# Input loads of the attention half of an encoder layer, issued by ScalarE instead of SyncE

## The chip, the cores and the metric

The kernel runs on one core of a Trainium2 chip. A core has a matrix engine (TensorE, PE in the profile, with its weight loads shown apart as PEld), a vector engine (VectorE, DVE), a scalar engine (ScalarE, ACT), a general engine (GpSimd, POOL) and an engine that only issues transfers and waits (SyncE, SP). Each works through its own list of instructions in order; semaphores tie the lists together. Transfers between the core's memory and HBM are run by 16 DMA engines, and an engine's list holds the instruction that issues a transfer, with the waits in front of it.

The metric is device time in microseconds (us) from start to end of one execution; lower is better. Before the change the median of three runs is 1496.47 us (1496.44 to 1498.27).

## The reference, cut to what matters

One layer of a streaming encoder, 1024 positions by 1024 channels, float32. Two kinds of attention run side by side on one normalised input and are joined by one output projection; then a gated MLP follows.

```python
mod = jnp.dot(jax.nn.silu(c), w_ada[l]) + b_ada[l]
sh_a, sc_a, g_a, sh_m, sc_m, g_m = jnp.split(mod, N_MOD, axis=-1)
h = modulate(rmsnorm(x, g_attn_norm[l]), sh_a, sc_a)
proj = jnp.dot(h, w_in[l])
q_lat, kv_lat, k_rope, ca_qkv = jnp.split(proj, split_pts, axis=-1)
q = jnp.dot(rmsnorm(q_lat, g_q_latent[l]), w_q_up[l]).reshape(B, S, MLA_HEADS, MLA_QK)
kv = jnp.dot(rmsnorm(kv_lat, g_kv_latent[l]), w_kv_up[l]).reshape(B, S, MLA_HEADS, MLA_NOPE + MLA_V)
...
o_mla = mla_attention(q, k, v)                       # 8 heads, chunk-causal, all earlier keys
...
o_ca = chunk_attention(cq, ck, cv, rel_bias[l])      # 8 heads, band of 9 chunks of 64 keys, bias
mixed = jnp.dot(jnp.concatenate([o_mla, o_ca], axis=-1), w_out[l])
x = x + g_a[:, None, :] * mixed
h = modulate(rmsnorm(x, g_mlp_norm[l]), sh_m, sc_m)
u = causal_dwconv(jnp.dot(h, w_up[l]), conv_w[l], conv_b[l])
gate, val = jnp.split(u, 2, axis=-1)
x = x + g_m[:, None, :] * jnp.dot(jax.nn.silu(gate) * val, w_down[l])
```

Inputs x and c, the positions and all weights come from HBM; the result goes back to HBM.

## The kernel before, in words

**Arithmetic.** Every large product keeps float32 accuracy by splitting both operands into a rounded high part and a low remainder and adding three matmuls (`gemm3`, lines 146 to 152; its lines 150, 151 and 152 are the matmuls of most rows of the profile). So each weight that is loaded raw is then split: ACT writes the high part (`hi_of`, line 75), POOL or DVE subtracts it for the low part (`lo_of`, line 82). The raw buffer is free again when that subtraction is done.

**Stages.** (1) 0 to about 65 us: x is loaded and normalised, the first modulation rows are computed, and the query/key projection of the first pair of heads runs. (2) To about 105 us: the rotary tables (`rope_tables`), on DVE. (3) About 105 to 435 us: the banded attention, four pairs of heads. (4) About 435 to 690 us: the latent attention (`mla`), eight heads. (5) To about 790 us: output projection, residual, second normalisation. (6) The MLP, to the end, with its own loads at lines 978, 1023 and 1027.

**The attention loop.** `Unit.scores` (line 636) does 128 queries of one head: score matmuls (line 658), a minimum over the row on DVE (673 or 677), the exponential on ACT (683), the reciprocal and scale on DVE (685, 686), the probabilities as a float16 high part on POOL (helper line 71) and a low part on DVE (703), and then a transposing transfer issued by SP (705). `Unit.values` (709) multiplies the transposed tile with the values (716); it comes `DEPTH` = 3 tiles later. At the end of a group of four tiles the head's output goes to HBM (line 725, SP). There are three transpose buffers (`PT_BUFS` = 3).

**Work put between the tiles.** `pace` (line 805) takes steps from a list of fillers, which give PE work while a tile waits for the other engines: value and query/key projections (`f_v`, `f_qk`, by `load_w`), the latent projections (`f_m`, also by `load_w`), their up-projections (`f_up`), and the output projection of the four finished banded head pairs (`f_oca`). A side list, `f_ada` (419), computes three more modulation rows: 96 loads of 128 KB (line 426), each followed by one multiply-add of DVE (lines 428 and 430).

**The loads that the change touches** (all on SP before), with the buffer that each waits for:

- line 184 in `load_w`: 64 loads of projection weights into a ring `wr` of three buffers;
- line 263: the positions, once;
- line 426 in `f_ada`: 96 loads, in a ring `A` of three buffers that also holds the running sum;
- line 454 in `gate_bcast`: 6 short bias rows (4 from `f_ada`, 2 from the MLP's `gate_row`);
- lines 526 and 532 in `f_up`: 6 loads of up-projection weights, and line 591 in `load_wo`: 16 loads of output weights of 256 KB, all in a ring `sq` of two buffers that the squares of the normalisation use as well;
- line 604 in `f_oca`: 16 loads of 256 KB, the banded heads' outputs, written to HBM earlier at line 725, in a ring `R` of four;
- line 733 in `load_bias`: 8 bias tables, a ring of two.

**What sets the order.** The program text gives the dependencies and priorities; the order of each engine's list is then made by a planner that plays the program through with modelled durations before it is built:

```python
with tile.TileContext(nc, schedule_with_timeline_sim=True) as tc, ExitStack() as ctx:
...
            with tc.high_priority(offset=OFF_S):
```

`high_priority` lifts the score, probability and value steps ahead of the fillers (lines 645, 684, 714). A load's place in its engine's list is thus where the planner expects its buffer to come free, and the list is then fixed.

Of the kernel before, what the change touches and what calls it, by code (L numbers as in the profile page):

```python
# [23 lines left out]
P = 128  # L24
# [38 lines left out]
def layer_kernel(ctx, tc, I, out):  # L63
# [3 lines left out]
    def f32(ap):  # L67
        return ap.bitcast(F32)
# [101 lines left out]
    def load_w(name, src, ncol, he="a", ssw=None):  # L170
        tiles = []
        for k in range(ND):
            if ncol <= 256:
                w = hw.tile([P, 2, 256], F32R, name=f"{name}s{k}", tag="ws", bufs=16)
                hi, lo = w[:, 0, :ncol], w[:, 1, :ncol]
            else:
                wh = hw.tile([P, 512], F32R, name=f"{name}h{k}", tag="ws", bufs=16)
                wl = hw.tile([P, 512], F32R, name=f"{name}l{k}", tag="ws", bufs=16)
                hi, lo = wh[:, :ncol], wl[:, :ncol]
            for c0 in range(0, ncol, 256):  # L180
                c = slice(c0, min(c0 + 256, ncol))
                raw = hw.tile([P, 256], F32, name=f"{name}r{k}_{c0}", tag="wr", bufs=3)
                rw = raw[:, :c.stop - c0]
                sp.dma_start(rw, src[:, k, c])
                if ssw is not None:
                    junk = qtile(f"{name}j{k}")
                    act.activation(junk[:, :c.stop - c0], rw, AF.Square, accum_out=ssw[:, k:k + 1])
                hi_of(he, hi[:, c], rw)
                lo_of("p", lo[:, c], rw, hi[:, c])
            tiles.append((hi, lo))  # L190
        return tiles
# [44 lines left out]
    for d in range(ND):  # L236
        if d + 1 < ND:
            load_ada(d + 1)
        w = wada[d]
# [20 lines left out]


    def rope_tables():
        sp.dma_start(pos_i[:], I["pos"])
        buf = [st.tile([P, 8, NT, 16], F32, name=f"rt{i}", tag="x", bufs=4) for i in range(8)]
        cnt = [0]

        def T():
            cnt[0] += 1
            return buf[(cnt[0] - 1) // 8][:, (cnt[0] - 1) % 8]

        def rnd(src, q):
            o = T()
            dve.tensor_scalar(o, src, q, MAGIC, op0=MUL, op1=ADD)
            dve.tensor_scalar(o, o, MAGIC, None, op0=SUB)
            return o

        def fma(n, c, b):
            o = T()
            dve.scalar_tensor_tensor(o, n, c, b, op0=MUL, op1=ADD)
            return o  # L280

        p1 = _grid(TWO_PI, 2.0 ** -9)
        p2 = _grid(TWO_PI - p1, 2.0 ** -21)
        p3 = TWO_PI - p1 - p2

        def reduce(src):
            n = rnd(src, 1.0 / TWO_PI)
            r = fma(n, -p1, src)
            r = fma(n, -p2, r)
            return fma(n, -p3, r)  # L290

        pf = cst.tile([P, NT], F32, name="pf")
        dve.tensor_copy(pf[:], pos_i[:])
        ang = T()
        dve.tensor_tensor(ang, pf[:].unsqueeze(2).to_broadcast([P, NT, 16]),
                          pk[:, C_INV:C_INV + 16].unsqueeze(1).to_broadcast([P, NT, 16]), op=MUL)
        nh = rnd(ang, 2.0 ** -20)
        rem = fma(nh, -(2.0 ** 20), ang)
        nm = rnd(rem, 2.0 ** -8)
        lo = fma(nm, -(2.0 ** 8), rem)  # L300
        tot = reduce(lo)
        for n, w in ((nh, 2.0 ** 20), (nm, 2.0 ** 8)):
            c = w - round(w / TWO_PI) * TWO_PI
            c1 = _grid(c, 2.0 ** -9)
            x = T()
            dve.tensor_scalar(x, n, c1, None, op0=MUL)
            x = fma(n, c - c1, reduce(x))
            y = T()
            dve.tensor_tensor(y, tot, x, op=ADD)
            tot = y  # L310
        tot = reduce(tot)
        pi_s = 3.1415925
        sn, cn, cl, c2, cl2 = T(), T(), T(), T(), T()
        dve.tensor_scalar(cl, tot, pi_s, -pi_s, op0=MIN, op1=MAX)
        act.activation(sn, cl, AF.Sin)
        dve.tensor_scalar(c2, tot, math.pi / 2, None, op0=ADD)
        dve.tensor_scalar(cl2, reduce(c2), pi_s, -pi_s, op0=MIN, op1=MAX)
        act.activation(cn, cl2, AF.Sin)

        for tab, c0 in ((tabq, C_RQ), (tabk, C_RK)):  # L320
            for half, trig in ((0, cn), (1, sn)):
                for j in range(2):
                    o = half * 32 + j * 16
                    dve.tensor_tensor(tab[:, :, o:o + 16], trig,
                                      pk[:, c0 + j * 16:c0 + j * 16 + 16].unsqueeze(1)
                                      .to_broadcast([P, NT, 16]), op=MUL)
# [92 lines left out]
    def f_ada():  # L419
        for m in (2, 3, 4):  # L420
            for n in range(4):
                acc = atile(f"aacc{m}_{n}")
                c0 = m * D + n * 256
                for k in range(ND):
                    w = atile(f"aw{m}_{n}_{k}")
                    sp.dma_start(w[:], I["w_ada"][k * P:(k + 1) * P, c0:c0 + 256])
                    if k == 0:
                        dve.tensor_scalar(acc[:], w[:], cs[:, 0:1], None, op0=MUL)
                    else:
                        dve.scalar_tensor_tensor(acc[:], w[:], cs[:, k:k + 1], acc[:], op0=MUL, op1=ADD)  # L430
                    if k % 2 and k < ND - 1:
                        yield 0
                yield 0
                yield 0
                pt = ps.tile([P, 512], F32, name=f"p_ada{m}_{n}", tag="mm", bufs=2)
                if m == 2:
                    gate_bcast(pt[:, :256], acc, c0, 256, atile)
                    g = atile(f"gab{n}")
                    act.activation(g[:], pt[:, :256], AF.Copy)
                    sp.dma_start(ga_d[:, n * 256:(n + 1) * 256], g[:])  # L440
                else:
                    for i in range(2):
                        pe.matmul(pt[:, i:i + 1], acc[:, i * P:(i + 1) * P], ones[:, 0:1], start=True, stop=True)
                    act.activation(modT[:, 3 if m == 3 else 2, 2 * n:2 * n + 2], pt[:, 0:2], AF.Copy)
                yield 0
        b = pk[:, C_B + 24:C_B + 40].rearrange("p (a b) -> p a b", a=2)
        dve.tensor_tensor(modT[:, 3, :], modT[:, 3, :], b[:, 0], op=ADD)
        dve.tensor_tensor(modT[:, 2, :], modT[:, 2, :], b[:, 1], op=ADD)
        dve.scalar_tensor_tensor(modT[:, 2, :], modT[:, 2, :], 1.0, pk[:, C_GM:C_GM + ND], op0=ADD, op1=MUL)

    def gate_bcast(pt, acc, c0, w, alloc):

        br = alloc(f"brow{c0}")
        sp.dma_start(br[0:1, :w], I["b_ada"][:, c0:c0 + w])
        dve.tensor_tensor(acc[0:1, :w], acc[0:1, :w], br[0:1, :w], op=ADD)
        pe.matmul(pt, ones[:], acc[:, :w], start=True, stop=True)

# [59 lines left out]
    def f_up(gr):  # L517
# [5 lines left out]
        wq = []  # L523
        for k in range(2):
            raw = qtile(f"wqr{gr}_{k}")
            sp.dma_start(raw[:, :384], I["w_qu"][gr][:, k, :])
            w = g4([P, 2, 512], F32R, f"wq{gr}_{k}")
            hi_of("a", w[:, 0, :384], raw[:, :384])
            lo_of("p", w[:, 1, :384], raw[:, :384], w[:, 0, :384])
            wq.append(w)  # L530
        raw = qtile(f"wkr{gr}")
        sp.dma_start(raw[:], I["w_kvu"][gr])
        ssw = cst.tile([P, 1], F32, name=f"sswm{gr}")
        junk = qtile(f"wkj{gr}")
        act.activation(junk[:, 0:256].rearrange("p (a b) -> p a b", a=4),
# [50 lines left out]
    def load_wo(k0, n, he, le):  # L586
        ws = []
        for k in range(k0, k0 + 4):
            raw = qtile(f"wor{k}_{n}")
            sl = slice(n * 512, (n + 1) * 512)  # L590
            sp.dma_start(raw[:], I["w_out"][k * P:(k + 1) * P, sl])
            w = g4([P, 2, 512], F32R, f"wo{k}_{n}")
            hi_of(he, w[:, 0], raw[:])
            lo_of(le, w[:, 1], raw[:], w[:, 0])
            ws.append(w)
        return ws

    def f_oca():
        for n in range(2):
            ws = load_wo(4, n, "a", "p")  # L600
            for t in range(NT):
                lo = rtile(f"cl{t}_{n}", (P, 4, P), F32R)
                hi = rtile(f"ch{t}_{n}", (P, 4, P), F32R)
                sp.dma_start(f32(lo[:]), oT_d[4:8, :, t * P:(t + 1) * P].rearrange("k p t -> p k t"))
                hi_of("a", hi[:], f32(lo[:]))
                lo_of("p", lo[:], f32(lo[:]), hi[:])
                pt = ps.tile([P, 512], F32, name=f"oc{t}_{n}", tag="mm", bufs=2)
# [122 lines left out]

    def load_bias(hd):
        b = apg.tile([P, 256], F32, name=f"bias{hd}", tag="bias", bufs=2)
        sp.dma_start(b[:], I["bias"][hd])
        dve.tensor_scalar(b[:], b[:], pk[:, C_RB + hd:C_RB + hd + 1], -1.0, op0=SUB, op1=MUL)
        dve.memset(b[0:64, 192:256], BIG)
        biases[hd] = b
# [381 lines left out]
```

## Time and profile before

| What | Value |
|---|---|
| median of three runs | 1496.47 us (1496.44 to 1498.27) |
| profiled execution, its own time | 1497.56 us |
| its span, from first to last instruction | 1495.8 us |
| mean granted TensorE clock | 0.918 of full speed |
| busy share of the span | PE 86%, PEld 71%, DVE 69%, ACT 41%, POOL 56% |
| transfers | 185.94 MB, nearly all on one queue, 43.0% of the 16 DMA engines' span |
| transposing transfers | 152 (64 in the banded, 88 in the latent attention) |
| loads of the lines listed above | 213 |

The page of the profile gives busy time by engine, the same in 40 slices, the DMA queues, the chain of work that ended last, the costliest groups of instructions and the transfers by line. "L426" is line 426 of the kernel; SPq is SP's list, whose time is all issuing and waiting, so it is not counted as busy. `aacc<-aw,cs,aacc` reads: the tile `aacc` is written from `aw`, `cs` and `aacc`. "Idle before, releaser" tells how long an engine stood still ahead of a group, and what ended that. A transfer's time to landing runs from the start of its issue to the last byte's semaphore, and holds no waiting in front of the issue.

### The profile page before, as it was taken

How to read it: one execution, taken by the hardware profiler on the slowest of the kernel's cores; microseconds unless marked ns; L12 is line 12 of the kernel's file. 1: busy time of each engine (PE TensorE's matmuls, PEld its weight loads, DVE VectorE, ACT ScalarE, POOL GpSimd, SP SyncE). 2: the span in 40 equal slices, each digit the busy share in tenths (PEclk: the TensorE clock that was granted, in tenths of full speed). 3: DMA queues.
4: the chain of work that ended last, by engine and by line, in shares of the span. 5: the costliest groups of instructions: out<-in, count | busy, mean ns of one | idle time of the engine just before them, and what ended most of it. 6: DMA issues, size and time to landing. Idle time of an engine off the chain costs nothing.

```text
span 1495.8 us, 20236 instructions
## 1 busy us (share of the span) xinstructions
PE 1283.1 (86%) x6836; PEld 1063.9 (71%) x6836; DVE 1037.7 (69%) x1710; ACT 617.5 (41%) x1190; POOL 841.8 (56%) x860
## 2 busy tenths in 40 slices
PE   3859989998968788876829769999999999999997
PEld 2759868976747666655617558888888887887885
DVE  6864786466768768863576658887787788556553
ACT  4454353343546545532444224444444443332331
POOL 4264453373799845443766146665565555665663
PEclk9979988998878899987958979999999999999999
DMA  7323656464512668778411242222222234446442
GB/s 275 134 70 73 135 121 143 116 134 102 124 49 53 145 144 167 163 156 287 149 74 57 71 143 82 85 85 85 85 85 84 77 129 169 148 148 234 154 141 99
DMA packets 217443, 185.94 MB, mean 124 GB/s; under 512 B 147958, under 2 KB 182906, under 8 KB 216316
## 3 DMA queue, kind: packets, MB, share of 16 engines
q1 hardware_dynamic: 217340, 184.66, 43.0%
q8 instruction: 54, 0.88, 0.2%
q14 instruction: 49, 0.40, 0.1%
HBM read 121.17 MB, written 28.84 MB: 100 GB/s over the span
## 4 chain that ended last, share of the span: by engine, by line
PE 48%; DMA 16%; DVE 13%; POOL 12%; issue 7%; ACT 2%; SPq 1%; DVEq 0%; POOLq 0%; ACTq 0%
PE p L964 7%; PE p L962 7%; PE p L963 7%; POOL wds L82 4%; DMA aw<-w_ada 4%; DMA PTm<-hlm 3%; PE sc L658 3%; PE dnp L1034 2%; PE dnp L1036 2%; PE dnp L1035 2%; DVE adacc L243 1%; DMA wu<-w_up 1%; PE ipv L150 1%; DVE aacc L430 1%; PE pvc L716 1%
## 5 line engine op out<-in xcount | busy, mean ns | idle before, releaser
L82 POOL TENSOR_TENSOR wds<-wd,wds 128x512 fp32r<-128x512 f32 x88 | 153.5, 1763 | 100.2 <-ACT wds L75 100.2
L1034 PE MATMUL dnp<-wds,g 128*128 128x512 f32 x308 | 119.9, 391 | 4.3 <-DVE xo L1042 2.4
L1024 DVE TENSOR_TENSOR wd<-wd,gmbc 128x1024 f32<-128x1024 f32 x44 | 69.4, 1578 | 77.7 <-DMA wd<-w_down 77.7
L1035 PE MATMUL dnp<-wds,g 128*128 128x512 f32 x308 | 119.7, 389 | 0.0
L1036 PE MATMUL dnp<-wds,g 128*128 128x512 f32 x308 | 118.5, 390 | 0.5 <-DVE g L82 0.5
L75 ACT ACTIVATE wds<-wd 128x512 fp32r<-128x512 f32 x88 | 54.6, 624 | 152.0 <-PE dnp L1036 149.6
L71 POOL TENSOR_SCALAR hlm<-Pm,rim 128x512 f16<-128x512 f32 (+4 forms) x88 | 61.7, 704 | 71.6 <-DMA PTm<-hlm 53.9
L703 DVE SCALAR_TENSOR_TENSOR hlm<-Pm,rim,hlm 128x512 f16<-128x512 f32 (+4 forms) x88 | 69.7, 795 | 31.7 <-POOL hlm L71 31.4
L71 POOL TENSOR_SCALAR hlc<-Pc,ric 128x640 f16<-128x640 f32 (+2 forms) x64 | 45.5, 713 | 77.9 <-DVE ric L686 38.7
L82 POOL TENSOR_TENSOR wc<-ws,wc 128x512 fp32r<-128x512 f32 x22 | 50.8, 2311 | 64.9 <-ACT wc L75 64.9
L82 POOL TENSOR_TENSOR wa<-wu,wa 128x512 fp32r<-128x512 f32 x22 | 35.9, 1633 | 91.1 <-ACT wa L75 91.1
L970 DVE SCALAR_TENSOR_TENSOR u<-c,pk,u 128x1023 f32<-128x1023 f32 x44 | 75.6, 1725 | 4.1 <-ACT u L969 4.1
L82 DVE TENSOR_TENSOR g<-gr,g 128x512 fp32r<-128x512 f32 x44 | 70.9, 1613 | 8.8 <-ACT g L75 8.8
L683 ACT ACTIVATE Pc<-sc,mc 128x640 f32<-128x640 f32 (+2 forms) x64 | 42.2, 659 | 83.6 <-DVE mc L673 66.9
L658 PE MATMUL sm<-mk,mq 96*128 96x512 f32 (+3 forms) x288 | 70.2, 378 | 7.0 <-ACT Pm L683 6.5
L716 PE MATMUL pvm<-PTm,vt 128*128 128x128 f16 x576 | 50.6, 242 | 29.4 <-DMA PTm<-hlm 25.3
L658 PE MATMUL sc<-k,q 64*128 64x512 f32 (+3 forms) x288 | 69.8, 370 | 5.6 <-ACT Pc L683 3.7
L430 DVE SCALAR_TENSOR_TENSOR aacc<-aw,cs,aacc 128x256 f32<-128x256 f32 x84 | 45.5, 541 | 41.8 <-DMA aw<-w_ada 41.2
L716 PEld LDWEIGHTS <-vt 128*128 128x128 f16 x576 | 41.2, 110 | 42.8 <-issue 40.0
L1034 PEld LDWEIGHTS dnp<-wds,g 128*128 128x128 f32 x308 | 57.8, 188 | 18.0 <-DVE xo L1042 3.3
L1036 PEld LDWEIGHTS dnp<-wds,g 128*128 128x128 f32 x308 | 57.8, 188 | 13.5 <-DVE g L82 1.4
L971 DVE SCALAR_TENSOR_TENSOR u<-c,pk,u 128x1022 f32<-128x1022 f32 x44 | 66.8, 1554 | 0.0
(352 smaller groups left out, 4350.8 us busy)
## 6 DMA issues: line engine op xcount, KB each, us to landing
wu<-w_up SPq DMA_DIRECT2D x44, 512.0 KB, 3.5
wd<-w_down SPq DMA_DIRECT2D x44, 512.0 KB, 3.5
aw<-w_ada SPq DMA_DIRECT2D x96, 128.0 KB, 2.3
g_d<-u SPq DMA_DIRECT2D x22, 512.0 KB, 2.6
gr<-g_d SPq DMA_DIRECT2D x44, 256.0 KB, 3.1
x<-x SPq DMA_DIRECT2D x16, 512.0 KB, 7.4
adaw<-w_ada_a SPq DMA_DIRECT2D x8, 1024.0 KB, 4.9
wq_r<-w_qk SPq DMA_DIRECT2D x32, 128.0 KB, 2.4
```

The lines of the kernel that those rows point to most:

```text
L71: pool.tensor_scalar(o, i, s, 1.0, op0=MUL, op1=MUL)
L82: (pool if eng == "p" else dve).tensor_tensor(o, i, f32(hi), op=SUB)
L658: last = pe.matmul(s[:, c:c + w], qpg[rs_, a, q], kpgs[kh][rs_, b, ko:ko + w], start=(a == 0 and b == 0), stop=(a == 1))
L703: dve.scalar_tensor_tensor(hl[:, w:2 * w], pp, ri[:], hl[:, :w], op0=MUL, op1=SUB)
L716: last = pe.matmul(u.pv[:, c], u.vst(j), mov, start=(x == 0), stop=(x == len(todo) - 1))
L962: pe.matmul(pt, sh, pg[:, 0], start=(k == 0), stop=False)
L963: pe.matmul(pt, sh, pg[:, 1], start=False, stop=False)
L964: pe.matmul(pt, sl, pg[:, 0], start=False, stop=(k == 3))
L970: dve.scalar_tensor_tensor(u[:, 1:], c[:, :S - 1], pk[:, cv + 1:cv + 2], u[:, 1:], op0=MUL, op1=ADD)
L1034: pe.matmul(pts[t][n], sh, w[n][:, 0], start=(j == 0), stop=False)
L1035: pe.matmul(pts[t][n], sh, w[n][:, 1], start=False, stop=False)
L1036: pe.matmul(pts[t][n], sl, w[n][:, 0], start=False, stop=(j == NF - 1))
```

## The change

Ten lines are edited, each in the same way: the engine that issues a load becomes ACT. The transfers, their sizes, their buffers and everything that reads them stay. On SP stay the loads of x and of the first modulation rows (lines 94, 199, 205), the transposes (705), the stores (440, 611, 725), and all transfers of the output stage and of the MLP but the two short bias rows of `gate_bcast`.

```diff
@@ load_w
-                sp.dma_start(rw, src[:, k, c])
+                act.dma_start(rw, src[:, k, c])
@@ rope_tables
-        sp.dma_start(pos_i[:], I["pos"])
+        act.dma_start(pos_i[:], I["pos"])
@@ f_ada
-                    sp.dma_start(w[:], I["w_ada"][k * P:(k + 1) * P, c0:c0 + 256])
+                    act.dma_start(w[:], I["w_ada"][k * P:(k + 1) * P, c0:c0 + 256])
@@ gate_bcast
-        sp.dma_start(br[0:1, :w], I["b_ada"][:, c0:c0 + w])
+        act.dma_start(br[0:1, :w], I["b_ada"][:, c0:c0 + w])
@@ f_up
-            sp.dma_start(raw[:, :384], I["w_qu"][gr][:, k, :])
+            act.dma_start(raw[:, :384], I["w_qu"][gr][:, k, :])
...
-        sp.dma_start(raw[:], I["w_kvu"][gr])
+        act.dma_start(raw[:], I["w_kvu"][gr])
@@ load_wo
-            sp.dma_start(raw[:], I["w_out"][k * P:(k + 1) * P, sl])
+            act.dma_start(raw[:], I["w_out"][k * P:(k + 1) * P, sl])
@@ f_oca
-                sp.dma_start(f32(lo[:]), oT_d[4:8, :, t * P:(t + 1) * P].rearrange("k p t -> p k t"))
+                act.dma_start(f32(lo[:]), oT_d[4:8, :, t * P:(t + 1) * P].rearrange("k p t -> p k t"))
@@ load_bias
-        sp.dma_start(b[:], I["bias"][hd])
+        act.dma_start(b[:], I["bias"][hd])
```

The planner runs again over the changed program, so the order of the other instructions can change too.

## The prediction

> **What bounds the kernel now.** I read the page first: busy shares, then the chain that ended last.
>
> ```profile
> PE 1283.1 (86%) x6836; PEld 1063.9 (71%) x6836; DVE 1037.7 (69%) x1710; ACT 617.5 (41%) x1190; POOL 841.8 (56%) x860
> PE 48%; DMA 16%; DVE 13%; POOL 12%; issue 7%; ACT 2%; SPq 1%; DVEq 0%; POOLq 0%; ACTq 0%
> ```
>
> PE carries the kernel. ACT, which is to get the loads, is the least busy engine and hardly on the chain. The MLP, from 790 us on, keeps its own loads on SP, so it can't move by more than its two short bias rows (line 454). I therefore read the table by stretches of time.
>
> ```profile
> core 0: us, PE busy (x) PEld busy (x) DVE busy (x) ACT busy (x) POOL busy (x), PEclk, DMA share, GB/s
> 60.00:690.00 630.00, 526.32 (x3500) 444.32 (x3499) 432.70 (x1167) 289.60 (x696) 356.59 (x528) 0.88 0.54 121
> 105.00:312.00 207.00, 199.02 (x1485) 177.39 (x1484) 134.58 (x394) 83.97 (x209) 93.36 (x117) 0.93 0.51 117
> 312.00:435.00 123.00, 102.46 (x584) 84.88 (x584) 82.48 (x235) 56.62 (x165) 82.78 (x163) 0.87 0.46 102
> 435.00:690.00 255.00, 198.00 (x1263) 158.66 (x1262) 182.35 (x442) 125.61 (x268) 155.12 (x222) 0.86 0.66 144
> ```
>
> From 105 to 312 us PE is idle for 8 us only: better loads can gain little there, worse ones can lose. From 312 to 690 us it is idle for 78 us. The clock column adds to that: stretches with gaps run slower.
>
> Next, SP's own waits from 60 to 690 us, the longest of them and one of line 184.
>
> ```profile
> SPq L705 <- DVE hlm L703: 48.0, 30, 10.1
> SPq L426 <- DMA aw<-w_ada: 44.4, 32, 3.1
> ...
> SPq L426 <- DVE aacc L430: 14.9, 24, 1.5
> SPq L184 <- POOL wq_s L82: 13.5, 16, 1.8
> ```
>
> The columns are total, times and longest. SP's list stands not only for transposes whose data isn't ready, but also for loads whose buffer isn't free: line 426 waits for the load before it to land, line 184 for POOL's subtraction. Added up over all rows of the moved lines this is 88.5 (L426), 37.3 (L184), 18.8 (L526), 7.6 (L591), 6.4 (L604) and 7.1 us (the rest): 166 us in 163 waits. These waits go with the loads.
>
> Last, what SP's order costs now: its list at 225 us, ACT's at the same time, and the chain at 508 us.
>
> ```profile
> 226.35 1.47 SPq L705 DMA_TRANSPOSE PTc<-hlc  x1
> 227.93 5.11 SPq L184 DMA_DIRECT2D wq_r<-w_qk  x5
> ```
>
> ```profile
> 230.76 0.42 ACT L75 ACTIVATE wq_s<-wq_r 128x256 fp32r<-128x256 f32 x1 [5.77 <-DMA wq_r<-w_qk]
> 231.47 0.42 ACT L75 ACTIVATE wq_s<-wq_r 128x256 fp32r<-128x256 f32 x1 [0.29 <-DMA wq_r<-w_qk]
> 231.79 0.78 ACT L683 ACTIVATE Pc<-sc,mc 128x640 f32<-128x640 f32 x1
> ```
>
> ```profile
> 508.22 1.23 SPq L705
> ...
> 509.55 4.22 DMA cl<-oT_d
> ...
> 513.86 0.64 ACT ch L75
> ```
>
> At 227.93 a load is issued behind a transpose; ACT stands 5.77 us for its landing with an exponential (683) behind. At 508 a load stands behind 1.23 us of transpose issue, on the chain itself.
>
> **The change part by part**, against the profiled execution's 1497.56 us (span 1495.8, 1.8 around it), which is 1.1 above the median.
>
> *Issuing on ACT.* 213 loads; on SP they took 90.6 us by its timeline (40.3 for L426, 25.2 for L184, 25.1 for the rest), 0.43 each; the shortest of L426 is 0.327, so 70 us at the least. 196 of them lie in 60 to 690 us: 84 us, 13% of ACT's time there; ACT's list goes from 46% to 59% taken. Most of it lies in ACT's idle time. An ACT instruction that meets an issue waits half of one, 0.21 us: 0.13 x 0.21 x 696 instructions = 20 us of delay. What share of it reaches the end? The chain passes through 59 of ACT's 696 instructions today (8.5%), and through 204 of DVE's 1167 (17.5%), DVE being busy 69%. With issues and waits ACT comes near DVE's load, so I take 17.5%: **+3.4 us**; ends 0 and +84 (all on the path).
>
> *Waiting on ACT.* No row shows ACT waiting for a buffer in front of a load. Queued behind such a wait stand the exponentials (683), the evacuations of PE's results (366, 410, 481, 553, 610, 621, 624) and the splits of weights; PE waits for the first two groups through its PSUM buffers, two each. If the 166 us come along, ACT stands 26% of the stretch, and an instruction that meets a wait has half of it left; I take L426's mean, 44.4/32 = 1.4, so 0.7: 0.26 x 0.7 x 696 = 127 us of delay, x 17.5% = **+22 us**. Lower end 0: the planner puts other ACT work ahead of each load, and DVE, which the exponentials wait for, stands in the same L426 loads already (41.2 us at line 430). Upper end +166, all of it on the path.
>
> *Loads no longer behind transposes.* A transpose holds SP's list for 1.24 us (median, latent) or 1.31 (banded), 152 of them. Gone are the 5.8 us at 227.93, and on the chain of the latent stage, which holds four `cl` and three `wor` loads, half a transpose each, 7 x 0.62 = 4.4. The landing itself (2.3 us for `aw`, 3.2 for `cl`, medians) stays. **-10 us**. Ends: 0 (ACT is late instead), and -105, ACT's 56 us and DVE's 49 of waiting for moved loads if all went.
>
> *Transposes no longer behind loads.* From DVE's last write to the issue they stand 133 us in sum over all 152, by the two lines' times; SP spends 27 of these on transfers other than transposes. The chain holds 18 of the 152: 27 x 18/152 = **-3 us**; ends 0 and -27. What is late next is the landing (3.3 us), which the same 16 engines serve.
>
> *The rest* (positions, bias tables, bias rows; 15 short issues) I put at nothing: the tables are loaded a head ahead. If that cover goes, it is a landing of 2.6 us, eight times: 21 us at most. The first 11 weight loads, before 60 us, I put at nothing too: DVE is busy there for 37.3 of the 40 us from 25 on, and PE waits for it. *The new order* of all lists is unknown; bounded by nothing in the trace, it is in the range.
>
> Sum: 3.4 + 22 - 10 - 3 = +12.4; 1497.6 + 12.4 = 1510.0; less 1.1: **1509 us**.
>
> One rule speaks against the change. The Trainium skill (Perfetto Trace Analysis, "DMA Instruction — HWDGE") says that the sequencers share one descriptor generator, locked for the time of an issue, and that this lock wait is in the profiled issue time. By it an ACT load that meets one of SP's transposes (152 x 1.27 = 193 us of 585, a third) would wait 0.6 us more: 40 us more on ACT's list, and by the share above some 2 us on the sum. With all loads on one queue no row here can show it.
>
> **Rivals.** *Relief* (not slower): SP's crowding was the true cost, and ACT's idle half takes the loads. For it: the 5.77 us wait, the `cl` rows on the chain, ACT's 54% idle time. Against: PE's 96% from 105 to 312 us. Price: waits 0, issues at ACT's own share 8.5% (+1.7), -10, -3, and the clock that follows:
>
> ```profile
> 220.00:230.00 10.00, 9.87 (x47) 8.62 (x45) 7.65 (x28) 2.32 (x6) 5.12 (x7) 0.50 0.84 161
> ```
>
> From 210 to 240 us PE works 26 us at about 0.55 of its clock; at full clock 14, so -12. Sum -23: **1473 us** with the median's offset; with half of the clock's part 1479, and with none 1485. It decides as soon as less than 73 of the 166 us (9.6 of the 22) come along.
>
> *Hidden anyway* (the change doesn't do what it says): the loads land when they did, since the buffer, not the queue, sets them: 60 of 97 L426 waits end with an `aw` landing or DVE's multiply-add, and 29 of 64 L184 loads go out 0.03 us after POOL's subtraction. ACT's idle time takes the issues. Time 1494 to 1499. A rule leads here too: the Trainium skill (DMA: Bandwidth & Descriptors, "Issuing engines are not separate DMA queues") says that issuing from several engines saves only the issue time, since all transfers share 16 engines. By that the saving is SP's 90.6 us of issue, off the path but for the chain's 1.23 us pieces; the landing of 2.3 us against an issue of 0.33 agrees.
>
> **How the numbers follow.** Forecast (ACT's waits outweigh SP's relief): 0.52, 1500 to 1540. Relief: 0.34, 1473 to 1493. Hidden: 0.14, 1494 to 1499. The forecast's own range is wide because its main term lies between 0 and 166 us; the whole range leaves out a tenth at each end: 1477 to 1537. About 0.2%, 3 us, is what a measurement can tell from no change: faster 0.34, same 0.14, slower 0.52.
>
> **What would show it.** Right: ACT's rows from 60 to 690 us show waits in front of exponentials and evacuations that end with DVE (430), POOL (82) or `aw` landings; ACT's share of the chain rises well over 2%; SP's waits at L705 alone remain; PE's idle time grows between 105 and 312 us. Wrong: ACT's wait for `wq_r`, `wor` and `cl` (line 75) falls with no new wait of its own, and PE's idle time of 78 us from 312 us on shrinks. Issue rows on ACT above 0.6 us would show the shared generator. A change of some us after 790 us would come from the new order alone, and be none of my steps.

## The result, and the profile after

After the change the median is **1503.81 us** (16 runs, 1497.4 to 1522.5), against 1496.71 us for the kernel before in the same comparison (16 runs, 1493.2 to 1500.8). The ratio is 1.0051, 95% interval 1.0034 to 1.0067: **slower by 0.5%, some 7.6 us**. One run, 1522.5 us, counts as slow and is left out of the ratio; the others end at 1516.8. The profiled execution took 1501.98 us, its span 1500.2, 4.4 more than before.

The page's busy shares and its chain, which answer to the first lines of the prediction:

```profile
PE 1284.6 (86%) x6836; PEld 1067.3 (71%) x6836; DVE 1053.3 (70%) x1710; ACT 615.8 (41%) x1190; POOL 844.1 (56%) x860
PE 52%; DMA 15%; POOL 12%; DVE 11%; issue 6%; ACT 2%; SPq 0%; ACTq 0%; DVEq 0%; POOLq 0%
```

PE does the same work. SP has left the chain (1% before), and ACT's 2% hasn't grown. The table by stretches, with the columns of the one before:

```profile
60.00:690.00 630.00, 525.53 (x3471) 444.77 (x3470) 439.82 (x1165) 284.08 (x689) 350.21 (x526) 0.87 0.53 115
105.00:312.00 207.00, 202.01 (x1489) 180.21 (x1488) 134.02 (x389) 83.30 (x206) 95.50 (x118) 0.92 0.52 117
312.00:435.00 123.00, 102.11 (x574) 83.80 (x573) 81.83 (x224) 53.73 (x159) 76.28 (x159) 0.85 0.46 101
435.00:690.00 255.00, 194.83 (x1248) 157.41 (x1248) 189.15 (x451) 124.08 (x271) 154.43 (x225) 0.87 0.61 129
```

From 105 to 312 us PE's idle time fell from 8.0 to 5.0 us; the dense stretch that I feared for lost nothing. From 312 to 690 us it rose from 77.5 to 81.1. Marks in the two traces say the same: the last banded value product ends 2.1 us earlier than before, the first latent score starts 3.6 later, the last one 13.7 later, the output stage gives back 9.3 of that, and the MLP starts 6.1 later. So in these two traces the loss shows behind 395 us, in the change from banded to latent attention and in the latent attention itself, and 6.1 us of it are left where the MLP starts.

SP's longest waits from 60 to 690 us, then ACT's rows for the moved loads, before and after (total, times, longest):

```profile
SPq L705 <- DVE hlc L703: 168.9, 43, 50.3
SPq L705 <- DVE hlm L703: 92.2, 34, 32.5
```

```profile
ACT wo L75 <- DMA wor<-w_out: 21.6, 11, 9.4
ACT wq_s L75 <- DMA wq_r<-w_qk: 19.1, 16, 5.8
ACT ch L75 <- DMA cl<-oT_d: 8.9, 10, 1.9
```

```profile
ACT wq_s L75 <- DMA wq_r<-w_qk: 15.4, 13, 3.5
ACT wo L75 <- DMA wor<-w_out: 9.3, 5, 3.8
ACT ch L75 <- DMA cl<-oT_d: 8.2, 8, 2.8
```

SP now waits for data, no longer for buffers of loads, and ACT waits 16.7 us less in these three rows (26.6 less over all its rows for moved loads). ACT's own standing in front of a load, counted as the gap ahead of each issue on its list, adds up to some 88 us over the whole span (58 of it at line 426), where SP stood 166 us by its waits from 60 to 690 us. This is such a place, on ACT's list of the changed kernel:

```profile
399.18 3.59 ACTq L426 DMA_DIRECT2D aw<-w_ada  x2
403.12 0.49 ACT L553 ACTIVATE uqr<-qu 128x384 f32<-128x384 f32 x1 [3.75 <-PE lt_ps L498]
```

Two issues of 0.3 us take 3.59: the second load waits for its buffer, with an evacuation (line 553) behind it. PE's last matmul for that evacuation ends at 401.24 us, so at most 1.9 of the 3.59 us can delay it. The mechanism of my second step is there. The experiments ask what it costs.

### The profile page after: what moved, and what is told of

It reads as the page before. It is cut to its first block, busy times and chain, and to the rows that moved or that the text cites. A ratio compares the mean times of both kernels' runs of the same rounds, so it can differ in the third digit from the quotient of the medians.

```text
span 1500.2 us, 20226 instructions
## 1 busy us (share of the span) xinstructions
PE 1284.6 (86%) x6836; PEld 1067.3 (71%) x6836; DVE 1053.3 (70%) x1710; ACT 615.8 (41%) x1190; POOL 844.1 (56%) x860
## 4 chain that ended last, share of the span: by engine, by line
PE 52%; DMA 15%; POOL 12%; DVE 11%; issue 6%; ACT 2%; SPq 0%; ACTq 0%; DVEq 0%; POOLq 0%
PE p L964 8%; PE p L963 8%; PE p L962 8%; POOL wds L82 5%; DMA PTm<-hlm 4%; DMA aw<-w_ada 3%; PE sc L658 3%; PE dnp L1034 2%; PE dnp L1035 2%; PE dnp L1036 2%; PE sm L658 2%; DMA PTc<-hlc 1%; DVE adacc L243 1%; PE pvm L716 1%; PE pvc L716 1%
## 5 line engine op out<-in xcount | busy, mean ns | idle before, releaser
L703 DVE SCALAR_TENSOR_TENSOR hlm<-Pm,rim,hlm 128x512 f16<-128x512 f32 (+4 forms) x88 | 74.9, 854 | 36.4 <-POOL hlm L71 36.3
L658 PE MATMUL sm<-mk,mq 96*128 96x512 f32 (+3 forms) x288 | 74.7, 391 | 9.5 <-ACT Pm L683 8.5
L971 DVE SCALAR_TENSOR_TENSOR u<-c,pk,u 128x1022 f32<-128x1022 f32 x44 | 72.0, 1672 | 0.0
L1034 PEld LDWEIGHTS dnp<-wds,g 128*128 128x128 f32 x308 | 57.8, 188 | 15.4 <-ACT wds L75 1.8
L1036 PEld LDWEIGHTS dnp<-wds,g 128*128 128x128 f32 x308 | 57.8, 188 | 15.1 <-DVE g L82 3.0
```

The lines of the kernel that those rows point to most:

```text
L658: last = pe.matmul(s[:, c:c + w], qpg[rs_, a, q], kpgs[kh][rs_, b, ko:ko + w], start=(a == 0 and b == 0), stop=(a == 1))
L703: dve.scalar_tensor_tensor(hl[:, w:2 * w], pp, ri[:], hl[:, :w], op0=MUL, op1=SUB)
L1034: pe.matmul(pts[t][n], sh, w[n][:, 0], start=(j == 0), stop=False)
L1036: pe.matmul(pts[t][n], sl, w[n][:, 0], start=False, stop=(j == NF - 1))
```

## The experiments

Three theories went into them. *Waits on ACT*: work queued behind a load that ACT can't issue yet is late (the forecast). *Two queues*: a transpose now shares the 16 DMA engines with loads of another queue, and lands later. *Only the order*: the planner wrote other lists, and these are worse by chance. Every ratio is against runs of the kernel before on the same chip.

**Parts of the change, each with the planner's own order.** `early` moves lines 184, 263, 426, 454 and 733, `late` lines 526, 532, 591 and 604, `aw` line 426 alone, `l184` line 184 alone, each in this way:

```diff
-                    sp.dma_start(w[:], I["w_ada"][k * P:(k + 1) * P, c0:c0 + 256])
+                    act.dma_start(w[:], I["w_ada"][k * P:(k + 1) * P, c0:c0 + 256])
```

`early`:

> Only the loads of the banded stage and the tables go to ACT (lines 184, 263, 426, 454, 733; 175 of the 213); lines 526, 532, 591 and 604 stay on SP. Theory W (ACT stands in front of loads whose buffer isn't free, 58 us at line 426 alone in the changed kernel): most of the cost is here, +5 to +8 us. Theory Q (two queues share the 16 DMA engines, so transposes land later, which matters where the chain runs through them, in the latent stage): 0 to +3 us. Theory P (the difference is what order the planner happens to lay): any sign, and early and late don't add up to the whole.

`late`:

> Only the loads of the latent stage and of the output weights go to ACT (lines 526, 532, 591, 604; 38 loads). W: 0 to +3 us, since ACT stands only 16 us in front of these. Q: +5 to +12 us, since 88 transposes of the latent stage then run beside 256 KB loads, with a mean landing above the 3.33 us of before. P: any sign. In all cases the output stage, 684 to 742 us before, should shorten by up to 9 us, as in the changed kernel, if its cause is that x and the kept sums are no longer issued behind output weights on SP.

`aw`:

> Only line 426 on ACT (96 loads of modulation weights, 31 us of issue and 58 us of standing in front of them on ACT in the changed kernel); all other loads stay on SP. Waits on ACT (the forecast's step): these 58 of 88 us carry most of the cost, so +5 to +9 us (0.35 to 0.6%), with the loss between 395 and 437 us and in the latent stage. Two queues beside each other delay the transposes: the loads of this line last to the end of the latent stage and are 96 of 213, so about half of the change's cost, +3 to +5 us, and transposes with a load in flight land about 0.6 us later than the others. Only the planner's order: any value from -3 to +10 us, and no tie between the size of ACT's standing and the result.

`l184`:

> Only line 184 on ACT (64 loads of projection weights; all but the first lie before 437 us). Waits on ACT: the small remainder of ACT's standing (some 9 of 88 us), so 0 to +2 us, or down to -4 us if the loads that go out earlier at the top of the banded stage shorten it. Two queues: transposes of the banded stage land later beside these loads, +2 to +4 us, and the latent stage stays as before. Only the order: any value from -3 to +10 us; a loss in the latent stage, in which none of these loads lies, can come from the order alone.

Measured: `early` 1.0067 (1.0037 to 1.0096), `late` 1.0012 (0.9991 to 1.0033), `aw` 1.0076 (1.0048 to 1.0103), `l184` 1.0052 (1.0032 to 1.0072). One line alone, 426, costs as much as or more than all the edits together (1.0051; there are nine of them, not ten as the section on the change has it), and line 184 alone as much as all of them. The parts don't add up: lines 426 and 184 alone make 1.28% together, and `early`, which holds both, 0.67%. `early` (+10 us) and `aw` (+11) lie at or above what the waits on ACT foresaw, and `late` (+1.8) within it. `l184` (+7.8) lies far above its 0 to +2, with ACT standing 18 us in front of its loads. Its loss is all there at the first latent score, 8.9 us late, and the last one is 8.9 us late too: the latent stage takes as long as before, as the two queues foresaw, but they put the loss at +2 to +4 us. The loss lies in the banded stage, where these loads lie, so where it lies doesn't tell the loads from the order. That the parts don't add up made the order worth a test.

**Other orders.** The same two kernels with another offset of the values' priority, which makes the planner write other lists:

```diff
-OFF_S, OFF_P, OFF_V = 400, 200, 200
+OFF_S, OFF_P, OFF_V = 400, 200, 260
```

`b260` and `b120` are the kernel before with 260 and 120, `a260` and `a120` the changed one.

`b260`:

> The kernel before with one planner number changed (OFF_V 200 to 260): the same instructions and queues in another order. W and Q: within 0.2% of before. P: it can move by as much as the change did, 7 us, either way.

`a260`:

> The changed kernel with the same planner number (OFF_V 260). W and Q: slower than the b260 kernel by 5 to 10 us, as the change was at OFF_V 200. P: the difference from b260 has any sign or size up to some 10 us.

`b120`:

> The kernel before with the offset of the values' priority at 120: the partner of the run above. All theories: within 3 us of the kernel before, as at 260 (-0.1 us); more than that, of either sign, shows that an order alone moves the time as much as the change did.

`a120`:

> The whole change under a third order: the offset of the values' priority is 120 in place of 200. To be read against the kernel before with the same offset. Waits on ACT or two queues: +5 to +9 us over its partner, as for the other orders (+7.6 and +2.0). Only the order: the difference from its partner may be of either sign, -6 to +10 us.

Measured: `b260` 0.9999 (0.9985 to 1.0013), `a260` 1.0018 (0.9997 to 1.0040); `b120` 1.0060 (1.0042 to 1.0078), `a120` 1.0064 (1.0044 to 1.0083). An order alone, with every load on SP, cost 0.6% at 120, as much as the change; all theories had put `b120` within 3 us. From its partner the changed kernel differs by +0.5% at 200, +0.2% at 260 and nothing at 120, each uncertain by 0.2 to 0.3%. The output stage shows how little of a stretch's time need come from the engine: it takes 57.8 us before and 48.5 after, but also 47.9 in `b260`, where nothing was moved. There the last latent score is 9.7 us late as well, and the MLP starts when it does before: an end of the latent stage that is so late need not be a loss, and the start of the MLP is the better mark.

**The order held.** The next two kernels take engine and order apart. All instructions but the 213 loads are tied, list by list, to the order of another kernel, so that only a place for each load is left to the planner. The traces bear this out: without the 213 loads, the lists of all engines are the same, instruction by instruction, as those that they were tied to, while the changed kernel's DVE list departs from the one before in about 600 of 1710 places.

```diff
+    for row in zlib.decompress(base64.b85decode(ORDER)).decode().split(";"):
...
+            if last is not None:
+                tc.add_manual_dep(i, last.name, info, reason="order")
```

`new_eng_old_order` is the changed kernel with the lists of the kernel before; `old_eng_new_order` is the kernel before with those of the changed one.

`new_eng_old_order`:

> The whole change (213 loads on ACT), but every other instruction of all five engines is held in the order in which it stands in the kernel before; only the loads' places in ACT's list are new (the planner's). Waits on ACT (88 us of standing in front of loads) or two queues: the cost belongs to the loads themselves, so +5 to +9 us over the kernel before, as the change had (+7.6). Only the order: within 3 us of the kernel before, and 4 to 10 us faster than the changed kernel. Relief: 5 us or more below the kernel before, the order having hidden the gain.

`old_eng_new_order`:

> The other way round: all loads on SP as before, every other instruction in the order in which it stands in the changed kernel. Only the order: +5 to +9 us over the kernel before, with the loss between 395 and 437 us and in the latent stage, and the output stage some 9 us shorter. Waits on ACT or two queues: within 3 us of the kernel before, since SP stands in front of these loads again and no load shares the time with a transpose on a second queue; then 5 to 9 us below the changed kernel. Relief: above the changed kernel, since the order's cost stays and the gain is taken away.

Measured, with the kernel before and the changed one beside them:

| | order of before | order of after |
|---|---|---|
| loads on SP | 1 | 1.0349 (1.0325 to 1.0374) |
| loads on ACT | 1.0021 (1.0003 to 1.0038) | 1.0051 (1.0034 to 1.0067) |

With the order held, the moved loads cost 0.2%, some 3 us (0.5 to 5.7); from there the new order adds 0.3%, uncertain by some 0.24, so the two parts can't be ranked. The other way round it is +3.5% for the order and -2.9% for the loads: the split holds for one path only. None of the three theories foresaw that fourth corner: in the new order the loads must be on ACT, or 3.5% is lost. The new lists are made for loads that arrive early. ACT's list at the start of `old_eng_new_order`, and the same split in the changed kernel:

```profile
3.21 0.21 ACT L104 ACTIVATE cs<-pk 128x8 f32<-128x8 f32 x1 [1.20 <-DMA pk<-pack]
19.00 0.42 ACT L75 ACTIVATE wq_s<-wq_r 128x256 fp32r<-128x256 f32 x1 [15.59 <-DMA wq_r<-w_qk]
19.32 1.04 ACT L212 ACTIVATE xj<-x 128x1024 bf16<-128x1024 f32 x1
```

```profile
5.13 0.42 ACT L75 ACTIVATE wq_s<-wq_r 128x256 fp32r<-128x256 f32 x1 [0.18 <-issue]
```

On ACT the first weight goes out at 0.72 us, ahead of x; on SP it stands behind eight loads of x, and ACT's list, which has its split first, stands 15.59 us. Eleven of the 46 us by which this execution ends behind the changed kernel's are lost here; the rest comes in steps of 2 to 6 us along the attention. So "only the order" is too short as well: an order is good or bad for one placement of the loads.

With the order held, two traces can be laid side by side instruction by instruction. This shows what goes into the 0.2%. First, loads that now stand behind ACT's own work. ACT's list, before and in `new_eng_old_order`:

```profile
99.56 0.69 ACT L624 ACTIVATE k<-k_ps,gk_ca 128x512 fp32r<-128x512 f32 x1 [0.17 <-PE k_ps L618]
104.24 0.42 ACT L75 ACTIVATE wq_s<-wq_r 128x256 fp32r<-128x256 f32 x1
105.97 0.37 ACT L683 ACTIVATE Pc<-sc,mc 128x128 f32<-128x128 f32 x1
```

```profile
101.99 0.82 ACTq L184 DMA_DIRECT2D wq_r<-w_qk  x2
102.86 0.69 ACT L624 ACTIVATE k<-k_ps,gk_ca 128x512 fp32r<-128x512 f32 x1 [0.46 <-PE k_ps L618]
103.25 0.34 ACTq L184 DMA_DIRECT2D wq_r<-w_qk  x1
111.24 0.37 ACT L683 ACTIVATE Pc<-sc,mc 128x128 f32<-128x128 f32 x1
```

On SP these loads of line 184 went out one after the other from 91.10 us on. On ACT the load at 103.25 comes only when the evacuation of line 624 is through, which waited for PE; each load is chained to the split before it. The first exponential (683) slips from 105.97 to 111.24 us, and the median lag of DVE, ACT and POOL behind the kernel before grows here from 0.9 to some 4.5 us. Most of this is made up again: at 385 us the lag is 1.1 us. (The profiled execution of this kernel is a long one, 10.8 us over the kernel before where the medians differ by 3.5; such steps are read for their kind, not for their sum.)

Second, transposes that land later. The traces tell the landing of half to two thirds of the transposes and loads. Of the transposes whose landing both show, 33 have a load of ACT's in flight in `new_eng_old_order`: the same ones took 3.48 us on average before and 4.15 now. The 20 others took 3.20 and 3.31. In the other order (`old_eng_new_order` against the changed kernel) it is 3.34 to 3.73 for 60 with such a load, and 3.23 to 3.16 for 33 without. A transpose that lands late is also likelier to meet a load. But if only those count that were issued with a load already in flight, it is still 3.39 to 4.11 for 22, and 3.31 to 3.79 for 37 in the other order. On the chain from 60 to 690 us transposes went from 18 with 61.9 us to 24 with 98.4 in `new_eng_old_order`.

**Single parts with the order held.** The two remaining runs ask which loads bear the cost.

`aw_old_order`:

> Only line 426 on ACT (96 loads, the line before which ACT stands longest), every other instruction in the order of the kernel before. Free of the order, so against the +0.2% (+3.2 us) of all 213 loads in the old order. Waits on ACT: these 96 loads bring most of it or more, +3 to +8 us, in steps where ACT stands in front of an exponential or an evacuation. Two queues: +1 to +3 us, spread over the stretches in which these loads fly beside transposes; those transposes land some 0.6 us later than the same ones before, the others as before. Only the order: within 2 us, and at least 5 us below the same line on ACT in the planner's own order (+0.76%, +11 us).

`late_old_order`:

> Only the 38 loads of lines 526, 532, 591 and 604 on ACT, nearly all in the latent stage, every other instruction in the order of the kernel before. With all 213 loads on ACT in this order the profiled execution lost 6 us between 490 and 610 us. Two queues: most of these 6 us come back, +3 to +6 us, with transposes beside a load landing 0.4 to 0.7 us later than the same ones before. Waits on ACT: ACT stands some 10 us in front of these loads, so 0 to +2 us. Relief (the prediction's seven half transposes on the chain): -4 us.

Measured: `aw_old_order` 0.9982 (0.9967 to 0.9997), `late_old_order` 1.0013 (0.9995 to 1.0030). Line 426 is where ACT stands longest; it still stands 46 us in front of these 96 loads here, and the kernel is 0.2% *faster* than before. So in this order ACT's waits in front of line 426, the larger part of its standing, are no net cost, where that theory had +3 to +8 us. That is the net of two things. ACT's part of the chain from 60 to 690 us did grow, from 22.2 to 26.7 us (30.0 in `new_eng_old_order`); and DVE waits less for the same loads. Its rows for line 430, before and in `aw_old_order`:

```profile
DVE aacc L430 <- DMA aw<-w_ada: 41.2, 40, 3.2
```

```profile
DVE aacc L430 <- DMA aw<-w_ada: 32.5, 37, 2.7
```

The same line in the planner's order cost 0.76%: nearly one per cent between two orders of one program, some 14 us, where *Only the order* foresaw at least 5. The two-queue theory expected a loss, and is wrong here too on the sum, though not on the landings: 12 transposes beside a load of ACT's went from 3.13 to 3.77 us, the 57 others from 3.38 to 3.36. For `late_old_order` its +3 to +6 us came out as some +1.9, with 3.72 to 3.84 us for 20 transposes, less than expected; the waits on ACT, at 0 to +2 us, fit this run, though ACT stood 21 us and not 10.

Where a late landing meets the chain it shows at once. The chain of `aw_old_order`, of `late_old_order` and of the kernel before, at the change from banded to latent attention:

```profile
383.09 6.88 DMA PTc<-hlc
389.97 0.04 issue
390.01 1.22 PE pvc L716 x10
```

```profile
384.94 5.60 DMA PTc<-hlc
390.54 0.04 issue
390.58 1.23 PE pvc L716 x10
```

```profile
386.41 3.83 DMA wqr<-w_qu
390.24 0.02 issue
390.26 0.03 ACT wq L75
```

At that point `aw_old_order` was 5.0 us ahead of the kernel before; 1.4 of it are left behind the 6.88 us landing. `late_old_order` was 1.0 ahead and is 2.5 behind. In `new_eng_old_order` the transpose of the 6.88 us lands in 7.27, and 1.1 us of lag become 5.1; before, the same one landed in 3.89. Part of the difference is its issue, here on SP's list before and in `aw_old_order`; in `new_eng_old_order` it took 2.78 us:

```profile
388.10 1.51 SPq L705 DMA_TRANSPOSE PTc<-hlc  x1
```

```profile
383.09 2.13 SPq L705 DMA_TRANSPOSE PTc<-hlc  x1
```

Issues of over 2 us occur before too, with all loads on SP (up to 2.38), so no run shows that the second queue lengthened these.

By difference, 0.21 + 0.18 - 0.13, the 79 loads of lines 184, 263, 454 and 733 bear +0.26% (uncertain by some 0.3) with the order held, if the parts add up there. They weren't run alone in that order; the step at 100 us lies at line 184, but most of it was made up by 385 us.

`aw_old_order` is the fastest kernel of all, but its interval ends at 0.9997: the gain is barely told from none.

## Why the prediction was right and where it was wrong

The sign and the size came out near: +12.4 us forecast, +7.6 measured. The main term behind them was wrong, and some 0.3 of the measured 0.5% goes with the new order, which the sum left out. That the sum came out near was luck.

- **Waiting on ACT (+22): failed.** Two of its three factors were off. The time that comes along is 88 us, not 166. And the share that reaches the end isn't DVE's 17.5%: line 426 alone would be 22 x 88.5/166 = +11.7 us by that step, or +6.1 with the 46 us that ACT stood, and with the order held it gave -0.2%, some -2.7 us, relief included. The low end that I gave fits this: DVE stood for the same loads already, and waits 13 us less for them in `aw_old_order` (48.9 to 35.8 over lines 428 and 430). That ACT's work behind such a load seldom ends last isn't shown: ACT's part of the chain fell from 22.2 to 19.1 us in the changed kernel, but rose with the order held.
- **Issuing on ACT (+3.4): not seen.** The 213 issues took 75.8 us (0.36 each; I had 0.43 from SP's list). The 96 of `aw_old_order` left no loss.
- **Loads no longer behind transposes (-10): right in the view that I read it from, and taken up by transposes.** In the changed kernel SP's own part of the chain from 60 to 690 us fell from 12.4 to 2.1 us, and the four `cl` and three `wor` landings (26 us) left it. In their place came transposes: 18 on the chain with 61.9 us before, 20 with 83.3 after.
- **Transposes no longer behind loads (-3): the landing was left out.** "What is late next is the landing (3.3 us), which the same 16 engines serve", I wrote, and priced it at no change. The pairs put it at +0.1 to +0.7 us for a transpose with a load of the other queue in flight; what that comes to at the end wasn't measured apart.
- **The rest, at nothing.** The first loads cost 0.9 us at most. But I priced only compute behind loads, and not the opposite: loads of line 184 behind ACT's compute, some 3.5 us at 100 us, most of which was made up later.
- **The new order: "unknown, bounded by nothing", and not in the sum.** It is some +0.3% of the +0.5%; for line 426 alone it is 0.9%; an order with all loads on SP cost 0.6%. Only building other orders would have bounded it.
- **Smaller slips.** The 56 us of ACT's waiting in the upper end of relief is 69.7 by all its rows, and the tiles that lines 621 and 624 empty have one buffer, not two; neither is in the sum. The reading that stretches with gaps run at a lower clock fails in a finer row that the prediction shows itself: from 220 to 230 us PE was busy 9.87 of 10 us at 0.50. From 210 to 240 us it was busy 26.3 us at 0.54, and 27.3 us at 0.55 after the change, so the 12 us of clock that *Relief* counted on didn't come.

Of the signs that I named, ACT's waits in front of evacuations came; ACT's larger share of the chain and PE's longer idle time from 105 to 312 us didn't, in the changed kernel. Of the signs against, ACT's waits for `wq_r`, `wor` and `cl` fell, and PE's idle time from 312 us on grew. *Hidden anyway* (1494 to 1499 us, so within 2.5 of before) was nearest to the loads' own effect with the order held, for all of them (+3 us) and for line 426 alone (-2.7).

Both rules can be judged now. Of the shared generator nothing shows: 55 load issues of ACT that begin inside a transpose issue of SP take 345 ns (median), the 158 others 334, and a transpose's own issue takes 1.28 us (median) with a load issued beside it, 1.24 without. The Trainium skill (Perfetto Trace Analysis, "DMA Instruction — HWDGE") would have each wait for the other; the trace doesn't agree. Transfers of two issuers do lengthen each other, 3.48 to 4.15 us. The Trainium skill (DMA: Bandwidth & Descriptors, "Issuing engines are not separate DMA queues") says that they interleave on the same 16 engines, and the trace agrees; its other half, that only the issue time is saved, falls short of the places in both lists that shift with the engine.

What stays open: which pieces of the new order lose the 6.1 us that are left at the MLP, as no single wait was found to carry them; whether ACT's waits cost more in that order than with the order held; how the 0.2% divides between late landings and line 184; and whether the loads of line 184, alone and with the order held, are the whole of it.

## What to carry to other kernels

Where a planner writes the lists, an edit is two changes, the edit and a new order, and the second can be as large as the first or larger: hold the order of all other instructions and measure the edit alone, or try the edit under several orders, before explaining a change of under one per cent. A wait that moves to another engine need not cost anything: at line 426, where DVE stands for the same loads, it was no net loss in the one order in which it was measured alone. Moving loads to a second queue takes issues out of the way of transposes, and puts their bytes beside them: price the landing too.

## What the runs showed of the hardware

A transposing transfer that lands in 3.1 to 3.7 us on average took 0.1 to 0.7 us longer with a load from another engine's queue in flight, and 6.9 to 7.3 us in place of 3.89 at one crowded place on the chain. In the changed kernel the issue of a transpose on SP and of a plain load on ACT ran at the same time with little delay to either: medians of 1.28 us against 1.24 for the transpose, and 0.345 against 0.334 for the load.
